# Turning transposed pages in DRAM transfers instead of ScalarE copies, and an attention group as two tasks

## The chip, the cores and the metric

The kernel runs on one core of one Trainium2 chip. The metric is the time of one execution in microseconds of device time. Three runs of the kernel before took 2697.59, 2699.80 and 2701.71 us; their median, 2699.8 us, is the time to compare with.

## The reference

A two-layer encoder trunk over 256 tokens of width 4096, in float32:

```python
for l in range(DEPTH):                                    # DEPTH = 2
    h = rmsnorm(x, norm_w[l])
    proj = h @ w_in[l]                                    # 4096 -> 11264
    aq, ak, av, ag, rq, rk, rv, rg = jnp.split(proj, SPLIT_POINTS, axis=-1)
    # attention: 16 query heads in 4 groups, 4 key heads, head width 128
    aq = apply_axial_rope(rmsnorm(aq, q_norm[l]), rope) * attn_scale
    ak = apply_axial_rope(rmsnorm(ak, k_norm[l]), rope)
    a_out = jax.nn.silu(ag) * gqa_attention(aq, ak, av)
    # retention: 8 heads, key width 128, value width 256, decaying both ways
    rq, rk = apply_axial_rope(rq, rope), apply_axial_rope(rk, rope) * ret_scale
    r = bidirectional_retention(rq, rk, rv, log_gf, log_gb)
    r_out = jax.nn.silu(rg) * rmsnorm(r, ret_norm[l])
    x = x + jnp.concatenate([a_out, r_out], axis=-1) @ w_out[l]
return rmsnorm(x, final_norm)
```

## The kernel before

**Products.** Every float32 operand is split into a high and a low part of TensorE's rounded float32 type, and `product` (line 732) makes each product of three matmuls: high by high (line 734), high by the moving operand's low part (735), low by high (736). The large matmuls write 128x512 into the PSUM tiles M.

**Blocks.** Per layer, 11 blocks of the input projection and 4 of the output projection, each 1024 columns wide, so 30 blocks in all. A block (`block`, line 1049) goes through 16 pairs of 128-row slices of the contraction. Four pairs (SEVEN) use a seven-product scheme that needs sums of operands (x7h, x7l, from xf), the others an eight-product scheme (x8h, x8l and a difference). `combine` adds the PSUM tiles into two result pages, ca and cb. The order of the input blocks is: attention keys and values; four times an attention gate with its queries (ag, aq); then twice retention keys with queries (rk, rq) and two blocks of retention gates with values (rg, rv).

**Weights.** They stream from DRAM all the time: SP loads wraw (line 369), ScalarE casts whi from it, VectorE subtracts to make wlo. Five loads and five split pages are in flight. One page in ten is "far": ScalarE makes fhi and a negated copy, and POOL adds the weights to it with an accumulating transfer (flo, line 444).

**Other work.** Everything between the products is written as Python generators ("tasks" and "lanes") whose steps are put into the instruction streams between two products by a planner: `tick` (683) asks `Weights.room` (446) whether the steps still fit before the split weights run out, with a cost for each engine and due times (LANDING for a transfer, MARGIN, EARLY). The order thus made is fixed at build time; on the chip each engine runs its own stream in order and waits on semaphores. Of the tasks, one runs at a time, or two when the first is in its tail (`running`, 671). Pages of 128x1024 floats come from one pool of nine.

**Transposes.** Results have tokens on partitions; the next use needs features there. `transposed` (706) lets VectorE transpose the 32x32 blocks of a page in place (room), and ScalarE then puts the blocks where they belong, with 16 copies from 32 partitions to 32 partitions, in four steps of four. 58 pages go through it: gates, queries, keys, softmax rows, retention results and the residual. The transpose is ordered in the same step as whatever comes before it in the caller:

```python
ve.transpose(room.rearrange(flat), src.rearrange(flat))
yield rest
for i in range(4):
    for j in range(4):
        ac.copy(to[b, :, :, i, :], fr[a, :, :, j, :])
    yield
```

**Attention.** `attention_group` (872) is one task from the block's result to the mixed page: the gate, rotary embedding of the queries (`rotary`, 759, with the tables of `rope_tables`, loaded into the tile tables), and two `attention_pair`s (822) of two heads each: scores into a PSUM tile ps, softmax rows into pr (exponential, then a scaling by the reciprocal sums), transpose of pr, split into pTh and pTl, product with the values, product with the gate. Keys and values reach it through DRAM (kv_dram), the retention keys and queries as split halves through rk_dram and rq_dram. `put` (571) stores finished pages in next_dram, from where they are fetched (full, line 600) and split into operands (`split_pair`, 476) for the next products; the last two pages of eight stay in SBUF.

Of the kernel before, what the change touches and what calls it, by code (L numbers as in the profile page):

```python
# [17 lines left out]
P = 128  # L18
# [28 lines left out]
LANDING = 9.0  # L47
FAR_LANDING = 14.0
MARGIN = 0.4

EARLY = 0.7
# [3 lines left out]
SEVEN = (0, 4, 8, 12)  # L55

# [84 lines left out]
def is_far(group, p, k):  # L141

    return (p, k) == (group[2], PAGE_B)
# [60 lines left out]
def hybrid_encoder(  # L204
# [24 lines left out]
    next_dram = tc.dram_tile([NCH, P, KG * SEQ], F32, name="next_dram")  # L229
    x2_dram = tc.dram_tile([N_OUT, P, MT * NB], F32, name="x2_dram")  # L230
    kv_dram = tc.dram_tile([4, P, 4, SEQ], F32R, name="kv_dram")
    rk_dram = tc.dram_tile([4, P, 2, 2, SEQ], F32R, name="rk_dram")
    rq_dram = tc.dram_tile([4, P, 2, 2, SEQ], F32R, name="rq_dram")
# [8 lines left out]
    held = [0]  # L242

    def drop(n=1):

        held[0] -= n

    def page(shape, name, dt=F32):

        held[0] += 1  # L250
        return sp.tile(shape, dt, tag="pg", name=name, bufs=PAGES)
# [7 lines left out]
    junk = t(cp, [P, NB], "junk", dt=mybir.dt.bfloat16)  # L259
# [4 lines left out]
    def load_small():  # L264
        nc.sync.dma_start(dec, decay.partition_broadcast(P))

# [207 lines left out]
    late, waiting, stored, sums_of = [], [], set(), []  # L474

    def split_pair(p, v, l=None):
# [3 lines left out]
        def high(to, src):  # L480
            if not gains:
                ac.copy(to, src)
            for i, g in enumerate(gains):
                ac.activation(to[:, i, :], src[:, i, :], AF.Copy, scale=g)

        def low(to, src, hi):
            if not gains:
                ve.tensor_sub(to, src, f32(hi))
            for i, g in enumerate(gains):
                ve.scalar_tensor_tensor(  # L490
                    to[:, i, :], src[:, i, :], g, f32(hi)[:, i, :], op0=ALU.mult, op1=ALU.subtract
                )

        if p in SEVEN and gains:
            for i, g in enumerate(gains):
                ac.activation(v[:, i, :], v[:, i, :], AF.Copy, scale=g)
            yield
        x0, x1 = v[:, :, :P], v[:, :, P:]
        if p in SEVEN:
            while sums_of:  # L500
                yield
            sums_of.append(p)
            hi = t(ap, [P, 7, P], "x7h", len(SEVEN), F32R)
            lo = t(ap, [P, 7, P], "x7l", len(SEVEN), F32R)
            f = t(ap, [P, 5, P], "xf", 1)
            s1, s2, s3, s4, a22n = (f[:, i - S4, :] for i in (S1, S2, S3, S4, A22N))
            ac.activation(a22n, x1[:, 1, :], AF.Copy, scale=-1.0)
            ac.copy(hi[:, 0:2, :], x0)
            yield
            ve.tensor_sub(s1, a22n, x1[:, 0, :])  # L510
            ve.scalar_tensor_tensor(s2, s1, -1.0, x0[:, 0, :], op0=ALU.mult, op1=ALU.subtract)
            ve.tensor_sub(s3, x0[:, 0, :], x1[:, 0, :])
            ve.tensor_sub(s4, x0[:, 1, :], s2)
            yield
            ac.copy(hi[:, 2:7, :], f)
            ve.tensor_sub(lo[:, 0:2, :], x0, f32(hi)[:, 0:2, :])
            yield
            ve.tensor_sub(lo[:, 2:7, :], f, f32(hi)[:, 2:7, :])
            sums_of.pop()
        else:  # L520
# [3 lines left out]
            high(hi, v)  # L524
            yield
            low(lo, v, hi)
            ve.tensor_sub(x0, x0, x1)
            yield
            high(g[:, 0], x0)
            yield  # L530
            low(g[:, 1], x0, g[:, 0])
# [7 lines left out]
    def split_operand(c, l=None, rest=0.0):  # L539
        v, full[c] = full[c], None  # L540
        for k in range(2):
            p = 2 * c + k
            waiting.append(Lane(split_pair(p, v[:, 2 * k : 2 * k + 2, :], l)))
            waiting[-1].pair, waiting[-1].ready = p, now.t + rest
# [14 lines left out]
    def need(p, phase):  # L559

        while version[p] < phase:
            if coming(p, phase):
                split_step()
            elif turning and turning[0].step(True):
                pass
            elif late:
                split_late()
            else:
                advance()

    def put(c, v, l=None):

        full[c] = v
        if c >= NCH - 2:
            late.append((c, l))
        else:
            nc.gpsimd.dma_start(next_dram[c], v.rearrange("p k s -> p (k s)"))
            full[c] = None
            stored.add(c)
            drop()  # L580

    class Turn:
# [10 lines left out]
        def fetch(self, c):  # L593
# [4 lines left out]
            stored.remove(c)  # L598
            full[c] = page([P, KG, SEQ], "full")
            nc.gpsimd.dma_start(full[c].rearrange("p k s -> p (k s)"), next_dram[c])  # L600

        def step(self, forced=False):
            c = self.fetched
            if c < self.last and c < self.cut + 2 and (self.first or c in stored) and (held[0] < PAGES - 2 or not tasks):
# [8 lines left out]
            if self.cut == self.last:  # L613
                if self.first:
                    tasks.append(Lane(first_sums()))
# [23 lines left out]
    class Lane:  # L639
        def __init__(self, steps, heavy=True):  # L640
            self.heavy, self.tail = heavy, False
            self.steps, self.ready, self.last, self.done, self.value = steps, 0.0, 0.0, False, None

        def step(self):

            v, a = ve.until, ac.until
            rest = None
            try:
                rest = next(self.steps)
            except StopIteration as end:  # L650
                self.done, self.value = True, end.value
            if ve.until > v:
# [5 lines left out]
            if rest == "PE":  # L658
                self.ready = self.last + 2 * PASS
# [3 lines left out]
    def spawn(steps):  # L663
        lanes.append(Lane(steps))
# [5 lines left out]

    def running():

        return tasks[: 2 if len(tasks) > 1 and tasks[0].tail and not tasks[1].heavy else 1]

    def advance():

        clear()
        one = min(lanes + running(), key=lambda v: v.ready)
# [27 lines left out]
    def transposed(src, room, dst, rest=None):  # L706

        flat = "p m c -> p (m c)"
        ve.transpose(room.rearrange(flat), src.rearrange(flat))
        yield rest
        to = dst.rearrange("p i (m q b) -> p m i q b", m=MT, b=BLK)
        fr = room.rearrange("p m (i q b) -> p m i q b", i=4, b=BLK)
        for i in range(4):
            for j in range(4):
                a, b = slice(BLK * i, BLK * (i + 1)), slice(BLK * j, BLK * (j + 1))
                ac.copy(to[b, :, :, i, :], fr[a, :, :, j, :])
            if i == 3:  # L720
                drop()
            yield

# [8 lines left out]
    def product(out, a, b, start, stop):  # L732
# [4 lines left out]
        now.t += 3 * MM[out.shape[-1]]  # L737
# [21 lines left out]
    def rotary(v, L, kind):  # L759
# [5 lines left out]
        if kind in ("aq", "ak"):  # L765
            rs = t(sp, [P, 8], "rs", 2)
# [29 lines left out]
        oT = o.rearrange("p m (a s) -> p (m a) s", a=2)  # L796
        yield from transposed(o, v, oT)
        dst = parts_of(kind, [P, 4, SEQ])
        yield from split(dst, oT)
        drop()  # L800
        yield
        return (dst, rs) if kind == "aq" else dst
# [19 lines left out]
    def attention_pair(h, kv, qT, sgT, rs, rows_done):  # L822

        kT, v = (kv[:, 0, :], kv[:, 1, :]), [kv[:, i, :].rearrange("p (k d) -> p k d", k=MT) for i in (2, 3)]
        st = t(sp, [P, 2, 4], "st", 2)
        pr = page([P, MT, 2 * SEQ], "pr")
        for e in range(2):
            s = (yield from take_bank()).rearrange("p (m k) -> p m k", m=MT)
            for m in range(MT):
                product(s[:, m, :], at(qT, ALL, h + e, slice(m * P, (m + 1) * P)), kT, True, True)  # L830
            yield
# [16 lines left out]
            yield  # L848
        ve.reciprocal(st[:, 1, :], st[:, 1, :])
# [5 lines left out]
        rows_done.append(h)  # L855
        room = page([P, MT, NB], "room")
        prT = pr.rearrange("p m (a s) -> p (m a) s", a=2)
        yield from transposed(pr, room, prT)
        pT = parts_of("pT", [P, 4, SEQ])
        yield from split(pT, prT)  # L860
        drop()
        o = (yield from take_bank()).rearrange("p (e q) -> p e q", e=2)
        for e in range(2):
            for k in range(MT):
                product(o[:, e, :], at(v, ALL, k), at(pT, ALL, 2 * e + k), k == 0, k == MT - 1)
        yield
        drop(2)
        ve.tensor_mul(sgT[:, h : h + 2, :], o, sgT[:, h : h + 2, :])
# [3 lines left out]
    def attention_group(L, g, gacc, qacc):  # L872
        def gates():
            yield from gate(gacc, L)
            yield from transposed(gacc, page([P, MT, NB], "room"), sgT)

        kv = page([P, 4, SEQ], "kv", F32R)
        nc.gpsimd.dma_start(kv, kv_dram[g])
        sgT = gacc.rearrange("p m (a s) -> p (m a) s", a=2)
        one = spawn(gates())  # L880
        qT, rs = yield from rotary(qacc, L, "aq")
        while not one.done:
            yield
# [4 lines left out]
        yield from attention_pair(2, kv, qT, sgT, rs, done)  # L888
        while not one.done:
            yield  # L890
        drop(3)
        put(g, sgT)

    def retention_weights(L, i):

        kT = page([P, 2, 2, SEQ], "rk", F32R)
        qT = page([P, 2, 2, SEQ], "rq", F32R)
        nc.gpsimd.dma_start(kT, rk_dram[i])
        nc.gpsimd.dma_start(qT, rq_dram[i])
        dist = page([P, 2 * SEQ], "dist")  # L900
        nc.sync.dma_start(dist, consts[:, C_D:C_END])
        yield LANDING
        landed = max(now.t, L.stored) + LANDING
        D = page([P, 4, SEQ], "D")
        for e in range(2):
# [7 lines left out]
        drop()  # L913
        ac.activation(D, D, AF.Exp)
        yield max(landed - now.t, 0.1)
        for e in range(2):
            s = (yield from take_bank()).rearrange("p (k q) -> p k q", k=MT)
            for k in range(MT):
                product(
                    s[:, k, :],  # L920
                    (kT[:, 0, e, k * P : (k + 1) * P], kT[:, 1, e, k * P : (k + 1) * P]),
                    (qT[:, 0, e, :], qT[:, 1, e, :]),
                    True,
                    True,
                )
# [9 lines left out]
        L.weights[i] = wT  # L935
        yield
# [31 lines left out]
    def retention_pair(L, i, gacc, vacc):  # L968
        gain = page([P, NB], "gain")
        nc.sync.dma_start(gain, ret_norm[L.index, i * NB : (i + 1) * NB].partition_broadcast(P))  # L970
        v = yield from values(vacc, L)
        yield
        yield from gate(gacc, L, gain)
# [412 lines left out]
```

## Time and profile before

| | |
|---|---|
| median of three runs | 2699.8 us |
| profiled execution | 2701.46 us, span 2699.7 us |
| mean granted TensorE clock | 0.992 |
| TensorE busy | 2633.3 us (98%), 11832 matmuls |
| VectorE busy | 2068.9 us (77%) |
| ScalarE busy | 2025.1 us (75%) |
| POOL busy | 218.1 us (8%) |
| HBM traffic | 612.16 MB read, 30.41 MB written |

In the profile PE is TensorE, DVE VectorE, ACT ScalarE. A row of the stretch view gives, for a stretch of the span, each engine's busy time and in brackets its instructions; PEclk is the clock granted to TensorE as a share of full speed, DMA the mean busy share of the 16 DMA engines. A row of the group view ends with the idle time of the engine just before those instructions and with what ended it, after the arrow. In the order of time the same stands in square brackets. All vector and scalar instructions carry the line of a helper, so they are told apart by the tiles they write and read (out<-in).

### The profile page before, as it was taken

The page shows a single profiled execution, that of the slowest core. Times are in us where ns is not written, and L with a number is a line of the kernel's source. Part 1 is how long each engine was busy: PE and PEld are TensorE (multiplying, and loading weights), DVE is VectorE, ACT ScalarE, POOL GpSimd, SP SyncE. Part 2 cuts the span into 40 slices and gives each one's busy share as a digit, 9 for nine tenths or more (in the row PEclk, how much of TensorE's full clock was granted, in tenths as well). Part 3 has the DMA queues.
Part 4 walks back from the last instruction along what each step waited for, and adds up shares of the span by engine and source line. Part 5 has one row for each costly group of instructions (what it writes and reads, how often), then busy time and mean ns, then how long its engine had stood idle before and what let it go on. Part 6 is the DMA issues. An engine that isn't in the chain of part 4 may idle for free.

```text
span 2699.7 us, 34139 instructions
## 1 busy us (share of the span) xinstructions
PE 2633.3 (98%) x11832; PEld 2182.0 (81%) x11832; DVE 2068.9 (77%) x2489; ACT 2025.1 (75%) x3176; POOL 218.1 (8%) x278
## 2 busy tenths in 40 slices
PE   6999999999999999999999999999999999999997
PEld 5878788788888888888788878887888888888886
DVE  8777787678787797766888767787778778986766
ACT  6768898887776778766987788888867777775554
POOL 0010000000100110001011100000000101000000
PEclk9999999999999999999999999999999999999998
DMA  7876677667877887888788867776678779778885
GB/s 250 279 234 218 210 223 230 202 211 231 271 247 221 286 261 223 262 257 265 266 255 246 252 191 231 212 221 209 216 244 256 238 236 306 239 221 250 248 254 183
DMA packets 191149, 644.82 MB, mean 239 GB/s; under 512 B 20736, under 2 KB 27904, under 8 KB 190976
## 3 DMA queue, kind: packets, MB, share of 16 engines
q1 hardware_dynamic: 150208, 525.19, 56.4%
q0 software_dynamic: 40768, 117.46, 19.9%
q8 instruction: 92, 1.51, 0.2%
q14 instruction: 81, 0.66, 0.1%
HBM read 612.16 MB, written 30.41 MB: 238 GB/s over the span
## 4 chain that ended last, share of the span: by engine, by line
PE 79%; DVE 7%; ACT 5%; issue 4%; DMA 4%; SPq 0%; POOL 0%; DVEq 0%; POOLq 0%; ACTq 0%
PE M L735 26%; PE M L734 25%; PE M L736 25%; DVE wlo L189 4%; DMA wraw<-in_w_in 3%; ACT pr L189 2%; ACT whi L189 2%; DMA wraw<-in_w_out 1%; PE ps L736 1%; PE ps L734 1%; PE ps L735 1%; DVE ca L189 0%; DVE cb L189 0%; DVE wsum L189 0%; ACT fhi L189 0%
## 5 line engine op out<-in xcount | busy, mean ns | idle before, releaser
L189 DVE TENSOR_TENSOR wlo<-wraw,whi 128x1024 fp32r<-128x1024 f32 x842 | 946.5, 1143 | 251.2 <-ACT whi L189 245.0
L189 ACT CAST whi<-wraw 128x1024 fp32r<-128x1024 f32 x842 | 815.2, 988 | 396.4 <-PE M L736 291.8
L735 PE MATMUL M<-wlo,x8h 128*128 128x512 f32 x1806 | 705.8, 391 | 3.3 <-DVE wlo L189 3.3
L734 PE MATMUL M<-whi,x8h 128*128 128x512 f32 x1806 | 706.1, 391 | 1.1 <-DVE ca L189 1.1
L736 PE MATMUL M<-whi,x8l 128*128 128x512 f32 x1806 | 704.8, 390 | 0.0
L735 PEld LDWEIGHTS M<-wlo,x8h 128*128 128x128 f32 x1806 | 340.8, 189 | 73.6 <-DVE wlo L189 4.1
L734 PEld LDWEIGHTS M<-whi,x8h 128*128 128x128 f32 x1806 | 340.7, 189 | 72.5 <-DVE ca L189 2.4
L736 PEld LDWEIGHTS M<-whi,x8l 128*128 128x128 f32 x1806 | 340.5, 189 | 71.5
L189 DVE TENSOR_TENSOR wlo<-wsum,whi 128x1024 fp32r<-128x1024 f32 x240 | 292.7, 1220 | 85.6 <-ACT whi L189 84.7
L189 ACT CAST whi<-wsum 128x1024 fp32r<-128x1024 f32 x240 | 252.0, 1050 | 121.2 <-PE M L736 108.3
L735 PE MATMUL M<-wlo,x7h 128*128 128x512 f32 x840 | 328.5, 391 | 10.5 <-DVE wlo L189 10.5
L736 PE MATMUL M<-whi,x7l 128*128 128x512 f32 x840 | 328.0, 390 | 6.0 <-DVE x7l L189 6.0
L734 PE MATMUL M<-whi,x7h 128*128 128x512 f32 x840 | 327.9, 390 | 0.1
L735 PE MATMUL M<-wlo,x 128*128 128x512 f32 x602 | 236.0, 392 | 12.8 <-DVE wlo L189 12.8
L734 PE MATMUL M<-whi,x 128*128 128x512 f32 x602 | 235.1, 390 | 11.6 <-ACT whi L189 11.6
L736 PE MATMUL M<-whi,x 128*128 128x512 f32 x602 | 235.0, 390 | 0.0
L189 DVE TENSOR_TENSOR wsum<-wraw 128x1024 f32<-128x1024 f32 x120 | 146.5, 1221 | 96.5 <-DMA wraw<-in_w_in 52.2
L735 PEld LDWEIGHTS M<-wlo,x7h 128*128 128x128 f32 x840 | 158.2, 188 | 44.6 <-DVE wlo L189 12.8
L736 PEld LDWEIGHTS M<-whi,x7l 128*128 128x128 f32 x840 | 158.2, 188 | 39.6 <-DVE x7l L189 6.7
L734 PEld LDWEIGHTS M<-whi,x7h 128*128 128x128 f32 x840 | 158.1, 188 | 33.5 <-DVE cb L189 0.7
L444 POOL DMA_DIRECT2D flo<-in_w_in x86 | 75.8, 881 | 1296.3 <-ACT flo L189 1086.6
L189 ACT CAST fhi<-wraw 128x1024 fp32r<-128x1024 f32 x118 | 124.2, 1052 | 73.6 <-PE M L736 64.8
(214 smaller groups left out, 3341.0 us busy)
## 6 DMA issues: line engine op xcount, KB each, us to landing
wraw<-in_w_in SPq DMA_DIRECT2D x703, 512.0 KB, 4.5
wraw<-in_w_out SPq DMA_DIRECT2D x256, 512.0 KB, 4.8
flo<-in_w_in POOLq DMA_DIRECT2D x86, 512.0 KB, 7.2
flo<-in_w_out POOLq DMA_DIRECT2D x32, 512.0 KB, 6.9
full<-next_dram POOLq DMA_DIRECT2D x18, 512.0 KB, 8.5
next_dram<-ca POOLq DMA_DIRECT2D x15, 512.0 KB, 6.1
x<-in_x SPq DMA_DIRECT2D x8, 512.0 KB, 7.1
kv<-kv_dram POOLq DMA_DIRECT2D x8, 512.0 KB, 7.8
```

Source lines behind the costliest of these rows:

```text
L189: return call(out, *args, **kwargs)
L444: self.adds.pop(0)[1]()
L734: nc.tensor.matmul(out, a[0], b[0], start=start, stop=False)
L735: nc.tensor.matmul(out, a[0], b[1], start=False, stop=False)
L736: nc.tensor.matmul(out, a[1], b[0], start=False, stop=stop)
```

## The change

Pages that are transposed are no longer put right by ScalarE. VectorE still transposes 32x32 blocks, in an order (`turned`) that lets four transfers (`store`, one for each 32 partitions) write the page to DRAM with the blocks in their places; whoever needs the page fetches it (`fetch`). 52 of the 58 pages go this way; the two last pages of each handover still use 16 ScalarE copies (`move`). The page now has tokens and features interleaved in runs of 32, so readers (`split_pair`, `split_turned`, `in_both`) use such patterns, the low parts with gains are split by token half, and the first layer's input is laid out so by the host. Attention is two tasks: `attention_group` makes gate and queries and stores them, `attention_rest` fetches them and does scores, softmax and values, with the softmax rows going through DRAM too. The scaled softmax rows and their transpose are now two steps. Retention keys and queries are stored once and split when they are fetched; the distance table stays in SBUF. The planner keeps account of pages that tasks will need (`need`, `pledged`), lets up to three tasks run, and has other constants.

```diff
-LANDING = 9.0
-FAR_LANDING = 14.0
-MARGIN = 0.4
-EARLY = 0.7
+LANDING = 8.0
+STORE, FETCH = 7.0, 10.0
+FAR_LANDING = 12.0
+MARGIN = 0.8
+EARLY = 1.0
+NEED = {"ak": 4, "ag": 3, "rk": 4, "rg": 4}
+PE_REST = 1.0
+AT_ONCE = 3
...
             for i in range(2):
-            low(lo, v, hi)
+                for m in range(MT) if gains else [ALL]:
+                    low(u[1][:, i, m], v[:, m, i], f32(u[0])[:, i, m], i)
...
             if rest == "PE":
-                self.ready = self.last + 2 * PASS
+                self.ready = self.last + PE_REST
...
+    def pledged():
+        return sum(max(0, v.need - v.own) for i, v in enumerate(tasks) if v.begun or not i)
...
     def running():
-        return tasks[: 2 if len(tasks) > 1 and tasks[0].tail and not tasks[1].heavy else 1]
+        one = [v for v in tasks if v.begun]
+        rest = [v for v in tasks if not v.begun]
+        if rest and len(one) < AT_ONCE:
+            need = held[0] + rest[0].need - rest[0].own + sum(max(0, w.need - w.own) for w in one)
+            if need <= PAGES:
+                one.append(rest[0])
+        return one
...
+    def turned(src, room):
+        ve.transpose(
+            room.rearrange("p (b k t) -> p b k t", b=4, t=BLK),
+            src.rearrange("p m (i b e) -> p b (m i) e", i=4, e=BLK),
+        )
+    def store(room, to):
+        to = to.rearrange("(b e) (a f) -> a e b f", e=BLK, a=4)
+        for a in range(4):
+            nc.gpsimd.dma_start(to[a], room[BLK * a : BLK * (a + 1), :].rearrange("e (b f) -> e b f", b=4))
+        drop()
+    def fetch(src, name):
+        v = page([P, KG * SEQ], name)
+        nc.gpsimd.dma_start(v, src)
+        return v
...
+        done.append(h)
         ve.reciprocal(st[:, 1, :], st[:, 1, :])
         yield
         for e in range(2):
             for m in range(MT):
                 w = pr[:, m, e * SEQ : (e + 1) * SEQ]
                 ac.activation(w, w, AF.Copy, scale=st[:, 1, 2 * e + m : 2 * e + m + 1])
-        rows_done.append(h)
-        room = page([P, MT, NB], "room")
-        prT = pr.rearrange("p m (a s) -> p (m a) s", a=2)
-        yield from transposed(pr, room, prT)
-        pT = parts_of("pT", [P, 4, SEQ])
-        yield from split(pT, prT)
+        yield
+        room = page([P, KG * SEQ], "room")
+        turned(pr, room)
+        drop()
+        yield 0.0
+        store(room, p_dram[2 * (g % 2) + h // 2])
+        yield STORE
+    def attention_values(g, h, kv, sgT):
+        v = [kv[:, i, :].rearrange("p (k d) -> p k d", k=MT) for i in (2, 3)]
+        pT = fetch(p_dram[2 * (g % 2) + h // 2], "pT")
+        yield FETCH
+        parts = parts_of("pT", [P, KG * SEQ])
+        yield from split(parts, pT)
         drop()
...
+    def attention_rest(L, g):
+        while g not in L.rs or now.t < L.kept:
+            yield
+        rs = L.rs.pop(g)
         kv = page([P, 4, SEQ], "kv", F32R)
         nc.gpsimd.dma_start(kv, kv_dram[g])
+        q = fetch(q_dram[g % 2], "q")
+        yield FETCH
+        qT = parts_of("aq", [P, 4, SEQ])
+        yield from split_turned(qT, q)
+        drop()
+        yield "PE"
         done = []
-        one = spawn(attention_pair(0, kv, qT, sgT, rs, done))
+        one = spawn(attention_pair(g, 0, kv, qT, rs, done))
         while not done:
             yield
+        two = spawn(attention_pair(g, 2, kv, qT, rs, done))
+        while len(done) < 2 or not one.done:
+            yield
+        pledge(5)
+        sgT = fetch(g_dram[g % 2], "sgT")
+        yield from attention_values(g, 0, kv, sgT)
+        while not two.done:
+            yield
+        yield from attention_values(g, 2, kv, sgT)
+        nc.gpsimd.dma_start(next_dram[g], sgT)
+        drop(2)
         put(g, sgT)
...
-            ve.tensor_scalar_mul(v, dist, lf)
+            ac.activation(v, dist, AF.Copy, scale=lf)
+            yield
...
-            ac.activation(junk, c[i][:, m, :], AF.Square, accum_out=sums[:, m, n : n + 1])
+            for k in range(2):
+                at_sum = n + 2 * k
+                ac.activation(
+                    junk, c[i][:, m, k * RV : (k + 1) * RV], AF.Square, accum_out=sums[:, m, at_sum : at_sum + 1]
+                )
```

More of the change, by code (lines that the diff above doesn't have):

```diff
@@ L561, in need @@
         while version[p] < phase:
-            if coming(p, phase):
+            if coming(p, phase) and not (short[0] and tasks):
                 split_step()
@@ L571, in put @@
     def put(c, v, l=None):
-        full[c] = v
         if c >= NCH - 2:
+            full[c] = v
+            own(-1)
             late.append((c, l))
         else:
[L577 to L580, printed above, removed]
+            stored[c] = now.t + LANDING
     class Turn:
@@ L874, in gates @@
             yield from gate(gacc, L)
-            yield from transposed(gacc, page([P, MT, NB], "room"), sgT)
+            room = page([P, KG * SEQ], "room")
+            turned(gacc, room)
+            drop()
+            yield 0.0
+            store(room, g_dram[g % 2])
+        yield from gates()
+        while "aq" not in L.tables:
+            yield
+        rs = yield from rotary(qacc, L, "aq", q_dram[g % 2])
+        yield STORE
+        L.rs[g] = rs
+    def attention_rest(L, g):
+        while g not in L.rs or now.t < L.kept:
+            yield
+        rs = L.rs.pop(g)
@@ L892, in attention_group @@
+        drop(2)
         put(g, sgT)
     def retention_weights(L, i):
[L896 to L903, printed above, removed]
+        while i // 2 not in L.stored:
+            yield
+        raw = page([P, 2, 4 * MT, 2 * BLK], "rkq")
@@ L904, in retention_weights @@
+        yield
+        for k in range(2):
+            for m in range(MT):
+                ve.tensor_sub(to[1][:, k, m], v[:, k, m], f32(to[0])[:, k, m])
+        drop()
         D = page([P, 4, SEQ], "D")
@@ L935, in retention_weights @@
         L.weights[i] = wT
+        own(-2)
+        pledge(0)
         yield
@@ L998, in keys_values @@
         drop(2)
-        L.tables["aq"] = rope_tables("aq", L.plain)
-        drop()
+        L.kept = now.t + LANDING
         yield
@@ L1041, in follow @@
         while finished:
-            if finished[0][0] == "M1" and (held[0] > PAGES - 2 or sum(v.heavy and not v.tail for v in tasks) > 1):
+            if finished[0][0] == "M1" and held[0] + pledged() > PAGES - 2:
                 if not now:
```

326 lines of the change are left out of this document (205 added, 121 removed).

## The prediction

> **What bounds the kernel now.** I read the page's span and engine shares first, then the busy time in 10 us and 84 us stretches, then who waits for whom, then the order of time around the worst waits.
>
> ```profile
> span 2699.7 us, 34139 instructions
> PE 2633.3 (98%) x11832; PEld 2182.0 (81%) x11832; DVE 2068.9 (77%) x2489; ACT 2025.1 (75%) x3176; POOL 218.1 (8%) x278
> ```
>
> TensorE is busy for 98% of the span: it is the bound. Both kernels order the same number of matmuls, so this change can win only what TensorE loses to waits and to a lowered clock. The profiled execution took 2701.46 us, 1.76 us over its span; the median of the runs is 2699.8, 1.66 us below that execution. I sum against 2701.46 and take the 1.66 off at the end.
>
> ```profile
> core 0: us, PE busy (x) PEld busy (x) DVE busy (x) ACT busy (x) POOL busy (x), PEclk, DMA share, GB/s
> 276.00:286.00 10.00, 7.12 (x25) 5.48 (x24) 6.07 (x6) 9.13 (x16) 0.00 (x0) 0.83 0.36 123
> 496.00:506.00 10.00, 7.60 (x34) 5.96 (x33) 6.25 (x6) 9.56 (x15) 0.86 (x1) 1.00 0.67 173
> 606.00:616.00 10.00, 8.34 (x37) 6.57 (x36) 7.04 (x8) 8.03 (x12) 0.86 (x1) 1.00 0.33 108
> 1604.00:1614.00 10.00, 7.12 (x25) 5.39 (x24) 6.86 (x7) 8.41 (x16) 0.00 (x0) 0.83 0.31 101
> 1826.00:1836.00 10.00, 7.58 (x27) 5.77 (x26) 7.61 (x8) 8.20 (x14) 0.86 (x1) 0.83 0.80 213
> 1937.00:1947.00 10.00, 8.37 (x37) 6.60 (x36) 7.83 (x8) 7.73 (x12) 0.86 (x1) 1.00 0.39 129
> 143.00:153.00 10.00, 4.95 (x14) 3.62 (x13) 6.58 (x14) 2.09 (x2) 2.00 (x1) 0.66 0.38 125
> 40.00:50.00 10.00, 4.33 (x11) 3.18 (x12) 9.22 (x17) 6.59 (x13) 0.00 (x0) 0.67 0.97 306
> 1300.00:1310.00 10.00, 7.17 (x25) 5.43 (x24) 7.70 (x13) 9.82 (x19) 0.00 (x0) 0.83 0.41 141
> 1400.00:1410.00 10.00, 10.00 (x46) 8.29 (x45) 7.83 (x15) 9.82 (x19) 1.00 (x2) 1.00 0.99 287
> ```
>
> The last row is TensorE undisturbed: 46 matmuls in 10 us, 0.217 us each. The other nine hold all its larger losses. The first six rows lie in attention, three in each layer; they are short by 21, 12, 9, 21, 19 and 9 matmuls, 91 in all, or **19.8 us**. The next three are the table loads (143), the start (40) and the end of an output block (1300): 32, 35 and 21 matmuls short, or 6.9, 7.6 and 4.6 us.
>
> ```profile
> 275.57 1.64 ACT L189 COPY pr<-room 32x256 f32<-32x256 f32 x4
> 278.19 1.71 ACT L189 ACTIVATE pr<-pr,st 128x256 f32<-128x256 f32 x4
> 279.93 1.25 DVE L189 STREAM_TRANSPOSE room<-pr 128x1024 f32<-128x1024 f32 x1 [5.00 <-ACT pr L189]
> 282.33 0.80 PE L735 MATMUL M<-wlo,x 128*128 128x512 f32 x1 [2.88 <-DVE wlo L189]
> 146.39 0.29 DVE L189 TENSOR_TENSOR C<-tables 128x128 f32<-128x128 f32 x1 [7.55 <-DMA tables<-in_k_norm]
> 148.61 0.79 PE L735 MATMUL M<-wlo,x7h 128*128 128x512 f32 x1 [5.05 <-DVE wlo L189]
> DVE room L189 <- ACT pr L189: 55.4, 14, 7.1
> PE ps L736 <- DVE aql L189: 2.7, 3, 1.0
> PE ps L734 <- DVE D L189: 1.4, 2, 1.0
> ```
>
> The mechanism in attention: ScalarE works through block copies (275.57) and reaches the scaling of the softmax rows late (278.19). The transpose of those rows has already been queued on VectorE in the same step; it blocks VectorE for 5.00 us, the weight split wlo stands behind it, and TensorE loses 2.88 us and then some clock (PEclk 0.83). Over the run that transpose keeps VectorE waiting 55.4 us. The pairs 5.00 to 2.88 and 7.55 to 5.05 also give the cushion: a blocked VectorE costs TensorE all but **2.1 to 2.5 us** of the block.
>
> ```profile
> 268.00:352.00 84.00, 81.12 (x362) 67.20 (x361) 60.74 (x68) 72.22 (x127) 6.33 (x7) 0.98 0.70 219
> 352.00:437.00 85.00, 85.00 (x398) 71.25 (x397) 67.14 (x81) 76.58 (x139) 6.25 (x7) 1.00 0.72 218
> ```
>
> It is not load alone: the second of these attention blocks has a busier ScalarE and no loss.
>
> **The change, part by part.** Block copies on ScalarE:
>
> ```profile
> 0.00:2700.00 2700.00, 49.67 (x40) 258.29 (x640) 0.99 0.77 239
> L189 ACT COPY rot<-cb 32x256 f32<-32x256 f32 x192 | 77.5, 404 | 4.2 <-DVE cb L189 1.6
> L189 ACT COPY rot<-ca 32x256 f32<-32x256 f32 x96 | 38.8, 404 | 4.5 <-DVE ca L189 3.3
> ```
>
> (The first row is all work that touches room.) 640 + 192 + 96 = 928 copies, 374.6 us. The new program keeps 96, 39 us. 832 copies, about 336 us, leave ScalarE; in an attention block it is 4 transposes of 16 copies at 0.404, 25.9 us, so ScalarE falls there from 72-77 us to some 46-51 of 84. The new scaling step also yields before the transpose is queued. I take all six attention losses as gone: **-19.8 us**. If the transpose still waits in half of them, half stays; that is in the range. What is late next is VectorE, at 61-67 us in these blocks, and the fetched pages below.
>
> The planner now waits 1.0 us, not 0.3, before it puts TensorE behind a split operand; the 2.7 + 1.4 us of ps waits above shrink: **-3.5 us**, between 0 and -4.1.
>
> Transfers. Each of 52 transposes becomes four 128 KB stores issued by POOL; 34 pages that used to stay in SBUF are fetched back (16 pT, 8 q, 8 sgT, 2 k), and the retention keys and queries travel once, not as two halves. One of the decay products moves from VectorE to ScalarE, 16 operations off the path: nothing, as ScalarE has just lost 336 us.
>
> ```profile
> L1010 POOL DMA_DIRECT2D rk_dram<-rkh x8: 554/565/574, 683.1 to 2222.8; - x8
> DMA to landing us min/median/max: 3.3/5.6/12.8
> DMA to landing us min/median/max: 3.0/7.0/16.7
> L189 DVE STREAM_TRANSPOSE room<-pr 128x1024 f32<-128x1024 f32 x16 | 19.9, 1244 | 55.4 <-ACT pr L189 55.4
> L736 PE MATMUL ps<-pTh,kv 128*128 128x256 f32 x64 | 18.1, 283 | 0.0
> q0 software_dynamic: 40768, 117.46, 19.9%
> 1360.00:1400.00 40.00, 39.51 (x173) 32.24 (x173) 33.32 (x45) 31.71 (x56) 5.05 (x6) 1.00 0.92 265
> ```
>
> (The two landing rows are those of rk_dram and next_dram, stores and fetches together.) The tightest chain is the first pair of heads of each group. The built order has 78 matmuls, 78 x 0.217 = 16.9 us, between its transpose and the ScalarE copy that reads the fetched page. The chain: transpose 1.24, four issues 4 x 0.565 = 2.26, landing 5.6, one issue 0.565, landing 7.0, together 16.7 us. It just fits; a copy late by less than the cushion costs nothing. Two fetches of k, and two of the second retention pair, which wait for a page that VectorE frees, are as tight. With both landings at their maxima the chain is 33.6 us, 17 late. I take **+2 us** for all of them, nearest the medians; the bounds are 0 and the second rival below. Behind a late fetch on POOL stand the far weight adds flo; behind a late copy on ScalarE stand the weight casts.
>
> DMA load: the software queue used 19.9% of 2699.7 us for 117.46 MB, 4.57 us of all engines per MB. An attention block gains 8 transfers of 0.524 MB, 4.2 MB, 19 us of 84: the share goes from 0.70 to about 0.93. At 0.92 (the 1360 row) TensorE lost 0.49 us of 40, which would be 8 us over 8 blocks: **+3 us**, between 0 and +8. POOL's 200 more issues at 0.565 are 113 us on an engine 8% busy: nothing, unless something waits in its queue.
>
> Start and tail.
>
> ```profile
> L189 DVE SCALAR_TENSOR_TENSOR x8l<-full,nw,x8h 128x256 fp32r<-128x256 f32 x42 | 18.4, 478 | 5.6 <-ACT x8h L189 5.6
> L189 DVE SCALAR_TENSOR_TENSOR x<-full,nw,x 128x128 fp32r<-128x128 f32 x42 | 12.7, 346 | 2.1 <-ACT x L189 2.1
> L189 ACT ACTIVATION_READ_ACCUMULATOR junk<-ca 128x1 f32 x32 | 6.0, 187 | 0.0
> ```
>
> With gains, a low part is four operations of 128, not two of 256: 4 x 0.346 - 2 x 0.478 = 0.43 us more of VectorE per pair. At 40:50 VectorE is 92% busy and TensorE waits for it; five pairs stand ahead of that wait: **+2.1 us**. Seven later pairs split under cover of TensorE's queued weights; without it they would cost 3.0 us more. The closing squares are split in two: two more of them with their reads on the last path, two reads of 0.187 and about as little of fixed cost: **+0.5 us**. The table wait at 143 and the wait at 1300 I leave as they are; the tables are loaded and used two weight pages earlier, on SP's queue and on VectorE's alike, and the 1300 stretch loses 2 of its 3 runs of block copies, so up to 4.6 us more may go there.
>
> Not shown before: VectorE's transpose with permuted reads and TensorE's moving operand in runs of 32. ScalarE's block copies already moved runs of 32 at 404 ns, so I take 0. Doubled, 58 transposes at 1.24 would add 72 us to VectorE, off the path, and the 192 matmuls that read pT, at 283 ns with some 0.11 between starts, 21 us on it.
>
> Sum: -19.8 - 3.5 + 2 + 3 + 2.1 + 0.5 = -15.7; 2701.46 - 15.7 = 2685.8, and 1.66 less in terms of the median: **2684 us**.
>
> **The rivals.** *Late fetches (slower).* Stores and fetches of a group share the software queue and the DMA engines with weights at 0.93. If the first pT of each of the 8 groups is 5 us late instead of 0, each costs 5 - 2.3 + 1.6 (the clock: 21 matmuls or 4.6 us lost at 276 against 2.88 idle), 4.3 us, 34 us in all: 2716. It decides from about 4.5 us on: 15.7 / 8 = 2.0 us each, plus the cushion. For it: the maxima 12.8 and 16.7. Against: the medians fit. [...]
>
> *The transfers eat the gain.* The full 8 us of DMA delay, half the attention waits kept (10 us) : 2684 + 5 + 10 = 2699, no change to be told. For it: 0.93 is above every attention row of before; against: 0.99 at 1400:1410 with no loss.
>
> [...]
>
> **How the numbers follow.** Forecast 0.66 (2669 to 2694), transfers eat the gain 0.14 (2694 to 2706), late fetches 0.16 and POOL 0.04 (2706 to 2730). A change of 0.2%, 5.4 us, is about the least that a measurement tells from none. Faster (below 2694.4): 0.66 and 0.04 of the second, 0.70. Slower (above 2705.2): 0.16 + 0.04 - 0.01, 0.19. Same: 0.11. The low end is 2684 less the 7 us of costs and some of the 1300 stretch, 2669; the high end takes in the second rival and half of the late fetches, 2712.
>
> **What would show it.** Right: no attention stretch of 10 us under 40 matmuls; VectorE waiting under 15 us for pr before its transposes; ScalarE near 1720 us; DMA share near 0.9 in attention; at 40:50 a wait about 2 us longer. Wrong: waits of ScalarE for pT, q, k or rkq of over 4 us each, with PE waiting for whi or wlo right behind; flo late; pT matmuls longer than 283 ns; VectorE's transposes over 1.3 us.

## The result and the profile after

The changed kernel takes **2669.3 us** (median of four runs, 2666.5 to 2671.7) against 2698.9 us of the kernel before in the same comparison: a ratio of 0.9889, 95% interval 0.9871 to 0.9906, or 29.6 us less. The forecast was 2684 us: 15.8 us less than 2699.8: right in sign, half in size. The profiled execution took 2666.53 us, the fastest of the four, while that of before was among its slowest, so the two profiles are 35 us apart.

The page of the changed kernel, span and engines:

```profile
span 2664.7 us, 33863 instructions
PE 2621.3 (98%) x11832; PEld 2177.8 (82%) x11832; DVE 2079.2 (78%) x2579; ACT 1724.6 (65%) x2426; POOL 336.7 (13%) x478
```

ScalarE is 300 us less busy, POOL issues 200 transfers more, and the same 11832 matmuls of TensorE take 12.0 us less. Most of that is the clock: by the trace's clock records, matmuls under a lowered clock lost about 10.7 us before and 3.1 us after. (The mean clocks, 0.992 and 0.996, also count a clock of 0.50 behind the last matmul, over 2686:2699 before and 2653:2664 after.) The stretches that answer to those of before, in 84 us of attention, at the end of an output block, at the table loads and at the start:

```profile
168.00:252.00 84.00, 84.00 (x375) 69.67 (x374) 65.75 (x73) 52.20 (x71) 13.15 (x18) 1.00 0.89 276
252.00:336.00 84.00, 84.00 (x392) 70.36 (x391) 66.92 (x78) 59.06 (x92) 17.67 (x27) 1.00 0.88 274
504.00:588.00 84.00, 84.00 (x394) 70.46 (x394) 65.99 (x81) 54.72 (x74) 12.50 (x20) 1.00 0.83 264
1270.00:1390.00 120.00, 118.50 (x522) 97.47 (x521) 103.10 (x174) 93.35 (x158) 16.80 (x24) 1.00 0.88 278
138.00:148.00 10.00, 4.37 (x13) 3.12 (x12) 5.49 (x14) 2.09 (x2) 2.12 (x1) 0.83 0.62 164
40.00:50.00 10.00, 4.99 (x16) 3.81 (x16) 9.42 (x21) 5.83 (x14) 0.00 (x0) 0.66 0.93 301
```

In attention TensorE no longer waits at all, with the DMA engines at 0.83 to 0.89 and ScalarE at 52 to 59 of 84 us. The table loads and the start are as they were. Who waited for whom, before (rows not shown above) and after; the numbers are total us, times, longest:

```profile
PE M L735 <- DVE wlo L189: 26.7, 15, 5.0
PE M L734 <- ACT whi L189: 11.6, 2, 11.1
PE M L736 <- DVE x7l L189: 6.0, 2, 5.0
PE M L734 <- DVE ca L189: 1.1, 3, 0.5
PE ps L734 <- ACT pr L189: 0.4, 2, 0.2
```

```profile
PE M L824 <- ACT whi L198: 9.4, 3, 8.9
PE M L825 <- DVE wlo L198: 8.5, 5, 5.6
PE M L826 <- DVE x7l L198: 6.3, 2, 5.0
PE M L825 <- DMA flo<-in_w_out: 1.2, 1, 1.2
PE M L825 <- DMA flo<-in_w_in: 0.4, 1, 0.4
PE M L824 <- DVE ca L198: 0.3, 1, 0.3
DVE room L198 <- ACT pr L198: 9.6, 16, 0.8
DVE C L198 <- DMA tables<-in_k_norm: 14.3, 2, 9.6
```

With the two ps rows that the prediction shows, TensorE waited 49.9 us before and 26.1 us after: 23.8 us. Those and the 12.0 us of busy time are 35.8 us; the tail takes 1.0 us back (below). Of the waits that are left, 8.9 us are the first weights and 5.6 us the tables.

### The profile page after: what moved, and what is told of

Same layout as the page of the kernel before. It is cut to its first block, busy times and chain, and to the rows that moved or that the text cites. A ratio compares the mean times of both kernels' runs of the same rounds, so it can differ in the third digit from the quotient of the medians.

```text
span 2664.7 us, 33863 instructions
## 1 busy us (share of the span) xinstructions
PE 2621.3 (98%) x11832; PEld 2177.8 (82%) x11832; DVE 2079.2 (78%) x2579; ACT 1724.6 (65%) x2426; POOL 336.7 (13%) x478
## 4 chain that ended last, share of the span: by engine, by line
PE 92%; DVE 3%; DMA 3%; issue 1%; ACT 1%; POOL 0%; SPq 0%; POOLq 0%; DVEq 0%; ACTq 0%
PE M L825 30%; PE M L824 30%; PE M L826 30%; DVE wlo L198 1%; PE ps L825 1%; PE ps L826 1%; PE ps L824 1%; DMA wraw<-in_w_in 1%; DMA ca<-in_x 0%; DMA flo<-in_w_out 0%; DMA flo<-in_w_in 0%; ACT whi L198 0%; DMA tables<-in_k_norm 0%; DVE cb L198 0%; DVE x8l L198 0%
```

## The experiments

Three theories: A, the order (a transpose queued right behind the scaling blocks VectorE); B, the load of ScalarE's block copies; C, the new planner.

**Order and load, one at a time and together.** The kernel before with the scaling and the transpose in two steps:

```diff
 rows_done.append(h)
+yield
 room = page([P, MT, NB], "room")
```

> The kernel before, with one thing changed: the scaling of the softmax rows and their transpose are two steps of the planner instead of one; all block copies stay on ScalarE. Theory A (order: the transpose queued right behind the scaling blocks VectorE): the six attention losses go, 2679 to 2684 us, VectorE's wait for pr falls from 55.4 to under 20 us. Theory B (load: ScalarE's 336 us of block copies make the scaling late): little moves, 2694 to 2699 us, the wait stays above 35 us. Theory C (the new planner: page account, three tasks, longer due times): 2694 to 2699 us, since nothing of it is here.

The changed kernel with the two in one step again:

```diff
-yield
 room = page([P, KG * SEQ], "room")
 turned(pr, room)
```

> The changed kernel with the scaling and the transpose put back into one step; nothing else. Theory A (order): VectorE's wait for pr goes back from 9.6 us to over 40, some six stalls return in attention, 2684 to 2690 us. Theory B (load): with ScalarE at 52 to 59 of 84 us the scaling is not late, the wait stays under 25 us, 2668 to 2674 us. Theory C (planner): 2668 to 2672 us.

The changed kernel with copies on ScalarE whose results nobody uses:

```diff
...
+def copies():
+    for i in range(4):
+        for j in range(4):
+            a, b = slice(BLK * i, BLK * (i + 1)), slice(BLK * j, BLK * (j + 1))
+            ac.copy(spare[b, :], dist[a, : 2 * P])
+        yield
...
 store(room, p_dram[2 * (g % 2) + h // 2])
+spawn(copies())
...
 store(v, to)
+spawn(copies())
```

> The changed kernel with ScalarE's load put back and nothing else: each of 34 stored pages (softmax rows, queries, keys) is accompanied by 16 copies of 32x256 between tiles that nobody else uses, in four steps of four, some 220 us in all. They are added work; the output does not use them. Theory A (order): the steps stay apart, so 2668 to 2676 us, no attention stretch of 10 us under 40 matmuls. Theory B (load): 2682 to 2690 us, attention stalls back. Theory C (planner): 2668 to 2674 us.

and both of these edits:

> The changed kernel with both put back, the copies on ScalarE and the single step. Theory A: as with the single step alone, 2684 to 2690 us. Theory B: as with the copies alone, 2682 to 2690 us. If each alone costs little and only this costs 15 us or more, the stalls need both, a late scaling and a transpose queued behind it. Theory C: under 2675 us.

Measured, with the ratio to the kernel before and its interval:

| | two steps | one step |
|---|---|---|
| no block copies (after, e2) | 2669.3, 0.9889 (0.9871 to 0.9906) | 2669.3, 0.9880 (0.9866 to 0.9895) |
| 34 pages with copies (e3, e4) | 2688.2, 0.9952 (0.9937 to 0.9966) | 2714.7, 1.0049 (1.0034 to 1.0064) |
| kernel before (e1, before) | 2685.4, 0.9941 (0.9924 to 0.9957) | 2698.9 |

Neither the order nor the load explains it alone. The single step costs nothing where ScalarE is free, 26.5 us where it is loaded; the load costs 19 us with two steps, 45 us with one. The rows say why. VectorE's wait for pr in e2 and in e4:

```profile
DVE room L198 <- ACT pr L198: 47.5, 16, 3.0
274.64 1.25 DVE L198 STREAM_TRANSPOSE room<-pr 128x1024 f32<-128x1024 f32 x1 [3.04 <-ACT pr L198]
336.00:420.00 84.00, 84.00 (x395) 70.46 (x394) 70.10 (x82) 58.48 (x93) 16.69 (x26) 1.00 0.86 268
```

```profile
DVE room L198 <- ACT pr L198: 65.1, 16, 6.2
PE M L835 <- DVE wlo L198: 35.7, 13, 4.7
282.51 1.25 DVE L198 STREAM_TRANSPOSE room<-pr 128x1024 f32<-128x1024 f32 x1 [5.12 <-ACT pr L198]
286.05 0.79 PE L835 MATMUL M<-wlo,x7h 128*128 128x512 f32 x1 [3.99 <-DVE wlo L198]
```

In e2 VectorE is blocked for 47.5 us, nearly as long as the 55.4 us of before, and TensorE loses nothing: sixteen blocks of 2.9 to 3.0 us, and each time TensorE runs on with the split weights that it has in stock. In e4 the sum is only 1.4 times as large, but eight of the sixteen blocks last 5 to 6 us, and all eight reach TensorE. The total of a wait says little; its longest says whether it can cost, though not how much. In the kernel before, the transpose behind this block

```profile
499.75 1.25 DVE L189 STREAM_TRANSPOSE room<-pr 128x1024 f32<-128x1024 f32 x1 [7.14 <-ACT pr L189]
```

kept VectorE for 7.14 us and cost TensorE 2.40 us (at 502.16, shown at the end), while 5.12 us cost 3.99 in e4. What two steps do under load, first VectorE's wait for pr in e1, then TensorE's waits and the worst attention block of e3:

```profile
DVE room L189 <- ACT pr L189: 18.2, 8, 4.2
```

```profile
PE M L835 <- DVE wlo L198: 13.5, 9, 5.6
PE ps L834 <- ACT aqh L198: 2.8, 2, 1.5
1676.00:1760.00 84.00, 80.88 (x375) 67.17 (x375) 64.04 (x76) 72.22 (x135) 16.62 (x26) 1.00 0.80 250
```

The long blocks are gone, but with ScalarE at 72 of 84 us TensorE still loses a few us in places, to late splits of weights and late casts of queries; its waits are 38.6 us in all, against 26.1. So e1 comes closest to theory A (1.4 us above its range) and e3 fits theory B. In e2 the time fits B and C, but the wait of 47.5 us is the one that A told (over 40; B told under 25). e4 fits none of the three. The stalls of before need a late scaling and a transpose queued right behind it; the load alone costs 19 us without them.

**The planner's times.** The changed kernel with 0.3 us instead of 1.0 before TensorE (`PE_REST = 2 * PASS`):

> The changed kernel with TensorE put behind a split operand after 0.3 us instead of 1.0 us, nothing else. The prediction's step (worth 3.5 us): the ps waits of before come back, 3 to 4 us in rows of PE ps behind VectorE's split, 2672 to 2674 us. Rival (the waits went because ScalarE and VectorE are no longer behind the planner's reckoning): no ps wait over 0.5 us, 2668 to 2671 us.

2672.9 us (2669.0 to 2674.9), 0.9895 (0.988 to 0.9909). The runs overlap those of the changed kernel; the profile shows one new group of ps waits, behind pTl (low parts of the softmax rows):

```profile
PE ps L825 <- DVE pTl L198: 1.7, 3, 0.9
```

All five old times:

```diff
-LANDING = 8.0
-FAR_LANDING = 12.0
-MARGIN = 0.8
-EARLY = 1.0
-PE_REST = 1.0
+LANDING = 9.0
+FAR_LANDING = 14.0
+MARGIN = 0.4
+EARLY = 0.7
+PE_REST = 2 * PASS
```

> The changed kernel with the five old due times: LANDING 9, FAR_LANDING 14, MARGIN 0.4, EARLY 0.7 and 0.3 us before TensorE. If the stalls of 1300 and 1360 went because of the wider margins, they come back and cost 5 to 10 us, 2675 to 2682 us. If they went with ScalarE's block copies, 2668 to 2673 us, with only the ps waits back.

2684.0 us, 0.9938 (0.9923 to 0.9953): half of the gain is lost, more than either forecast told, and at another place than 1300.

```profile
PE M L824 <- ACT x L198: 9.8, 2, 4.9
```

Once in each layer the first output block waits for the split of a mixed page that became ready too late, 4.9 us each time; the second matmul behind the first wait (at 1075.31) takes 0.63 us, where those ahead of the wait take 0.39. The table wait, though, is absent here (wlo waits of 2.6 us in all, not 8.5), so the old times also save something. Which of the five does what was not taken apart. Now the kernel before with two steps and the new MARGIN, EARLY and 1.0 us:

> The kernel before with the scaling and the transpose in two steps and the new MARGIN 0.8, EARLY 1.0 and 1.0 us before TensorE; block copies, one task at a time, LANDING and FAR_LANDING as before. If the second half of the gain (2685 to 2669 us) comes from these times, 2670 to 2677 us with no ps wait and no loss from 1290 to 1370. If it comes from ScalarE's block copies and the tasks, 2681 to 2687 us, with the ps waits alone gone.

2680.6 us (2680.3 to 2684.4), 0.9933 (0.9918 to 0.9948), 4.8 us below e1 by the medians, with intervals that overlap. So in the kernel before these times bring some 5 us of the 16 us between e1 and the changed kernel. The end of the first layer's output, before and in this run:

```profile
1290.00:1410.00 120.00, 115.66 (x498) 93.95 (x497) 99.06 (x151) 104.30 (x186) 12.85 (x17) 0.99 0.84 260
```

```profile
1290.00:1410.00 120.00, 111.36 (x479) 90.11 (x477) 92.39 (x135) 100.54 (x175) 11.38 (x15) 0.99 0.77 244
```

It lost 24 matmuls against the changed kernel's 522 before and 43 here. The changed kernel with copies for the six stored residual pages alone (`spawn(copies())` behind their store):

> The changed kernel with 16 copies of 32x256 on ScalarE put back for each of the six stored residual pages (layer 1 to 2), between tiles nobody else uses, in four steps of four; added work. If the losses of before at 1300 to 1364 (6.6 us, which the prediction left as they are) came from ScalarE's block copies there, they return: 2673 to 2678 us, TensorE losing 4 us or more between 1260 and 1370. If they went with the planner's new margins, 2668 to 2671 us.

2670.3 us (2668.0 to 2671.2), 0.9885 (0.987 to 0.99), no difference that the runs can tell. The profiles show none either. Between two fixed matmuls around this stretch (number 5270 and number 5800 of the 11160 that write M) lie 122.2 us in the changed kernel, 127.6 before, 128.8 in e1 and 130.9 in e13. In e9 it is 123.9, but in e10, e11, e12, e14 and e15, whose edits lie elsewhere, it is 124.5 to 126.7. So the residual copies are not shown to cost anything. The gain here is 5.4 us by the two profiles, of which only 0.9 us lies outside what versions of the changed kernel differ by among themselves. What brings it stays open; the tasks and their page account were not taken out alone.

**Transfers.** First copies of fetched pages placed 2 us after the issue, not 10 (`FETCH = 2.0`):

> The changed kernel with FETCH 2.0 instead of 10.0: the first copy of each fetched pT, q (24 pages) is placed 2 us after its transfer is issued, not 10, so ScalarE should wait for it some 4 to 5 us (landing 4.3 to 8.2 us). By the prediction's price of a late fetch (lateness less 2.3 us, plus 1.6 us of clock) 24 waits of 4.5 us cost 24 x 3.8 = 91 us, 2760 us. If ScalarE's lateness is mostly covered, because casts stand further ahead than VectorE's splits, 2670 to 2690 us. If FETCH is idle caution, 2669 us.

2751.4 us, 1.0186 (1.0168 to 1.0205).

```profile
ACT pTh L198 <- DMA pT<-p_dram: 59.2, 8, 9.2
ACT aqh L198 <- DMA q<-q_dram: 40.7, 8, 6.4
PE ps L824 <- ACT pTh L198: 38.4, 8, 6.6
```

Eight waits of 7.4 us and eight of 5.1. By the prediction's price, lateness less 2.3 plus 1.6, that is 8 x 6.7 + 8 x 4.4 = 89 us; measured are 82. The sum agrees, its parts do not: TensorE waits 44.2 us for pTh and pTl, and only 5.0 us for the queries' aqh and aql. Set against the changed kernel's trace matmul by matmul, a late pT costs about 8.4 us (6.7 by the price) and a late q about 2.0 (4.4 by the price). That they add up to nearly the same is luck. Nor was the place the one told. TensorE waits for pTh itself, since the planner puts its product there by the same clock, and not for whi or wlo. With 6 us (`FETCH = 6.0`):

> The changed kernel with FETCH 6.0 instead of 10.0 (2.0 cost 82 us). Fetched pages land 4.3 to 8.2 us after their issue, so the first copies wait some 1 to 2 us. With a cushion of 2.3 to 3 us they cost nothing: 2668 to 2674 us. If each late us costs its full length (24 waits of 1.5 us), 2700 to 2710 us.

2674.3 us (2672.0 to 2676.3), 0.9906 (0.9891 to 0.9921), 5 us more, with waits that are short:

```profile
ACT pTh L198 <- DMA pT<-p_dram: 9.0, 8, 2.0
PE ps L825 <- DVE pTl L198: 2.4, 3, 1.0
```

Waits of ScalarE up to 2.0 us give TensorE 2.4 us of waits in all. The rest of what TensorE waits more in this profile lies at places that this edit does not touch: the table wait is 7.9 us, not 5.6, and a flo wait 2.7 us, not 1.2. The table wait varies from 4.6 (e2) to 7.9 us (e12) in other runs that leave the tables as they are. A transfer of 0.524 MB more behind each fetch:

```diff
...
 nc.gpsimd.dma_start(v, src)
+spare.append(spare.pop(0))
+nc.gpsimd.dma_start(spare[0], src)
```

> The changed kernel with a second transfer of 0.524 MB behind each of its fetches, from DRAM to DRAM, that nobody waits for: 34 of them, 17.8 MB moved, some 10 us of all DMA engines per attention block, DMA share 0.83 to 0.89 up to 0.93 or more. By the prediction's price (+0.23 of share costs up to 8 us over 8 blocks) 2672 to 2677 us. If transfers cost nothing until weights come late, 2668 to 2671 us; if weights come late, more than 2680 us, with ScalarE waiting for wraw.

2670.0 us (2669.2 to 2671.3), 0.9886 (0.9872 to 0.9901): nothing.

```profile
168.00:252.00 84.00, 84.00 (x374) 69.58 (x373) 64.88 (x72) 53.04 (x71) 14.20 (x20) 1.00 0.93 298
```

At a share of 0.93, the one that the prediction feared, TensorE is busy for all of the 84 us.

**The start and the tables.** The first input page in four transfers, as before (`step = KG * SEQ // (KG if c == 0 else 1)`):

> The changed kernel with the first input page loaded in four transfers, as before, instead of two. If this is why its first matmul starts at 8.9 instead of 11.1 us, it starts at 10.5 to 11.5 us and the time is 2670 to 2672 us. If it is not, 2668 to 2670 us.

2671.9 us (2669.4 to 2675.2), 0.9893 (0.9878 to 0.9908); the runs overlap those of the changed kernel. The first matmul in the kernel before, in the changed one and in e12:

```profile
11.11 0.80 PE L734 MATMUL M<-whi,x 128*128 128x512 f32 x1 [11.11 <-ACT whi L189]
```

```profile
8.87 0.79 PE L824 MATMUL M<-whi,x 128*128 128x512 f32 x1 [8.87 <-ACT whi L198]
```

```profile
10.64 0.79 PE L824 MATMUL M<-whi,x 128*128 128x512 f32 x1 [10.64 <-ACT whi L198]
```

Here two issues on SP less ahead of the first weights make 1.8 of the 2.2 us. Over all profiles the first matmul starts at 8.7 to 10.0 us with two transfers (thirteen profiles) and at 10.4 to 11.1 with four (four profiles). Little of this lasts: matmul number 186 of those that write M starts at 66.7 to 69.8 us with two transfers and at 68.4 to 69.8 with four. The table loads moved ahead of the values' steps, with one page more pledged to the task:

```diff
-NEED = {"ak": 4, "ag": 3, "rk": 4, "rg": 4}
+NEED = {"ak": 5, "ag": 3, "rk": 4, "rg": 4}
...
+L.tables = {}
+L.plain = plain_tables(L.index)
 v = yield from values(vacc, L)
...
-L.tables = {}
-L.plain = plain_tables(L.index)
```

> The changed kernel with the four table loads of a layer's first task placed before the values' steps instead of behind them (and one page more pledged for it). The wait for the tables near 140 costs 7.4 us, 5.8 idle and the rest clock. If the loads only stand too late in SP's queue, they now go some 3 to 8 us earlier and the wait is under the 2.3 to 3 us that are covered: 2661 to 2664 us. If SP's queue is held by the weight loads before it whatever their place, little changes: 2666 to 2670 us.

**2661.6 us** (2660.5 to 2663.6), 0.9855 (0.984 to 0.987), the best of all: 7.7 us below the changed kernel. The first table load is issued at 122.3 us, not at 133.3. Where the changed kernel lost half of the stretch 138:148, TensorE is now busy throughout:

```profile
130.00:150.00 20.00, 20.00 (x90) 16.57 (x89) 18.92 (x30) 14.68 (x30) 5.34 (x5) 1.00 0.88 270
```

Waiting by plan instead (`yield 14.0` behind the loads):

> The changed kernel with 14 us of planned rest between the table loads and the first step that needs them, so that nothing of that task stands in VectorE's queue before the tables are there. By the order theory the wait of 9.6 us on VectorE goes, with it TensorE's 7.4 us: 2661 to 2664 us. If the loads slip with it or the delay is handed on to the queries, 2667 us or more.

2665.2 us (2662.0 to 2667.7), 0.9864 (0.9847 to 0.988): the wait on the tables is gone, but a wait on wlo of 2.6 us comes later. And the best version with FAR_LANDING 14:

> The version with the tables loaded earlier (2661.6 us) and FAR_LANDING 14 instead of 12, for the waits on flo near 1281 (1.7 us and what follows it up to 1305, some 5 us in all). If flo is planned too tightly, 2656 to 2660 us; if its lateness there has another cause (the end of the block, where everything is late), 2660 to 2664 us.

2661.9 us (2659.1 to 2664.2), 0.9859 (0.9842 to 0.9875): no gain. The flo wait of 1.5 us is 1.8 us here, so it does not hang on this planned time.

## Why the prediction was right in sign and half in size

- **Attention, -19.8.** Right, and about as large as told: 91 matmuls were missing, none is. VectorE's wait for pr fell to 9.6 us (told: under 15). Its reading, "it is not load alone", was right. What it did not see is how the two act together: with ScalarE free the single step costs nothing (e2), so the yield that it counted on was not needed here. ScalarE fell to 52 to 59 us of a block, not to 46 to 51. And the cushion of 2.1 to 2.5 us is no constant: in the same trace blocks of 7.14 and 6.06 us cost TensorE 2.40 and 1.66, all but 4.7 and 4.4.
- **The ps waits, -3.5.** They are gone whole: 2.7, 1.4 and 0.4 us, 4.5. Not shown to be the 1.0 us alone: with 0.3 us back only 1.7 us return, while in e13, with 1.0 us and two other new times, the aql waits fall from the 3.3 us of e1 to 0.4.
- **Late fetches, +2.** Mis-sized: 0. Neither ScalarE nor VectorE waits for pT, q or rkq. POOL does wait 42.5 us, up to 6.3 at a time, for stored rows to land before it fetches them as pT, and the planned times cover it. The chain was reckoned to just fit; the planned 7 and 10 us hold it, as e7 and e14 show for the 10 from the other side.
- **DMA load, +3.** Mis-sized: 0 in attention, and 0 again with 17.8 MB on top (e8). The 0.49 us that TensorE lost at 0.92 in the row of before were no measure of it.
- **Start, +2.1.** Not seen: x7l's longest wait is 5.0 us in both. At matmul number 186 of those that write M the changed kernel is 1.6 us ahead in these two profiles. The two loads of the first page, not a term of the sum at all, may have brought that, but versions with two loads differ by 3.1 us there.
- **The 1300 stretch, 0.** Mis-sized: 24 matmuls, 5.2 us, came back in this profile. The prediction named 4.6 us as possible and left them out of its sum. How much of it is the change and how much this one execution is open (behind e9).
- **Tail, +0.5.** 1.0: the last matmul starts 16.8 us before the end, now 17.7.

```profile
2682.94 0.39 PE L736 MATMUL M<-whi,x8l 128*128 128x512 f32 x1
```

```profile
2646.98 0.39 PE L826 MATMUL M<-whi,x8l 128*128 128x512 f32 x1
```

With these sizes, 2.2 us for the earlier first matmul and 0.6 for the longer table wait, the sum is -19.8 - 4.5 - 2.2 - 5.2 + 1.0 + 0.6 = -30.1. That this is near the 29.6 us of the medians is luck, since the sizes are read from two profiles that are 35.0 us apart. Set against each other matmul by matmul, with 0.113 us for each product that writes ps (an estimate, half of the 0.227 us from one start to the next of those that write M), the changed profile gains 1.6 us at the start, 26.8 in the attention of both layers with its ps waits, 5.4 in the 1300 stretch and 2.3 in all the rest, and loses 0.2 at the tables and 1.0 behind the last matmul: 34.9 us.

So the step that failed is the last of the working, the sizes of the costs. Late fetches (+2), DMA load (+3) and VectorE's low parts at the start (+2.1) stood in the sum with 7.1 us, and no run shows any of them. That is half of the 13.8 us by which the forecast fell short. The other half lies with gains that were set too small or at nothing: 1.0 us of ps waits, and the rest spread over attention, the 1300 stretch and the first page's loads. These runs do not share it out, since the last two vary by several us from one version to the next.

The rivals: late fetches did not come. Had the pT been late, e7 shows a price above the one told, 8.4 us for a wait of 7.4. Transfers do not eat the gain. The 2706 to 2730 us that had 0.04 for POOL did not come either: it issues a store in 550 to 602 ns with VectorE 78% busy:

```profile
L782 POOL DMA_DIRECT2D p_dram<-room x64: 550/567/602, 265.7 to 1856.6; - x64
```

The other signs came as told: ScalarE 1724.6 us (told 1720), DMA share 0.83 to 0.89 (told 0.9), products of pT 284 ns (283), transposes 1245 ns. One did not: the wait at 40:50 is no longer than before.

## What to carry to other kernels

An operation that waits at the head of an engine's queue cost nothing in these runs while the bound engine had finished work in stock (blocks of 2.9 to 3.0 us in e2), and a longer one cost time (5.12 us in e4 cost 3.99): read the longest of a group of waits, not its total, and ask how long a block must be to reach that engine. The stock differs from place to place (7.14 us cost 2.40 in the kernel before), so do not price every wait by one cushion. Two causes that each look sufficient may cost something only together, so take them out and put them in one at a time and both. Give costs that a planner's slack may cover their lower end unless a row shows the slack used up. Sizes read from one profile each are only as good as the spread between executions: compare the same matmuls in several. And when a kernel's large waits are gone, look at the loads that are issued late, which here were worth another 7.7 us by moving two lines and pledging one page.

## What the runs showed of the hardware

Waits of the same length sometimes came with a lowered clock of TensorE and sometimes didn't. Two of the kernel before, 2.40 and 2.42 us, with the matmul that ends the wait (the rows of the 10 us around them, 496 and 1826, stand in the prediction, with clocks of 1.00 and 0.83):

```profile
502.16 0.50 PE L735 MATMUL M<-wlo,x 128*128 128x512 f32 x1 [2.40 <-DVE wlo L189]
1830.72 0.50 PE L735 MATMUL M<-wlo,x 128*128 128x512 f32 x1 [2.42 <-DVE wlo L189]
```

So did two of e4, 2.25 us both, that end at 616.31 and at 1951.28:

```profile
611.00:621.00 10.00, 7.75 (x28) 5.97 (x27) 7.03 (x7) 9.78 (x18) 2.23 (x4) 0.83 0.58 188
1945.00:1955.00 10.00, 7.75 (x34) 6.11 (x33) 6.05 (x7) 9.76 (x18) 2.22 (x4) 1.00 0.63 189
```

With the lowered clock the 10 us hold seven matmuls less in the kernel before (27 against 34) and six less in e4 (28 against 34): at 0.217 us each, 1.5 and 1.3 us beyond the wait. A longer wait of e3, 3.12 us, lies in a stretch with a clock of 1.00 (1676:1760, shown above):

```profile
1716.62 0.50 PE L835 MATMUL M<-wlo,x7h 128*128 128x512 f32 x1 [3.12 <-DVE wlo L198]
```

So in these runs the length of a wait alone did not decide whether the clock fell. What else decided it is not shown.
